# Weight tiles that alternate between 0 and 64 mod 128 bytes, and new start addresses for attention's and the ConvFFN's operands

## The chip, the cores and the metric

The kernel runs on one NeuronCore of a Trainium2 chip. The metric is device time in microseconds from the start of the program to its end; lower is better. Engines are named as in the profile: PE is TensorE (PEld its weight loads), DVE is VectorE, ACT is ScalarE, POOL is GpSimd, SP is SyncE.

## The reference

One block of a hybrid encoder, batch 1, 512 frames (T), width 1024 (D), float32:

```python
h = rms_norm(x, norm_mix_g)
proj = h @ w_in + b_in                                  # 1024 -> 4864 (38 blocks of 128)
y_a = rwkv7_branch(proj[..., :1792], ...) @ w_branch_a  # 8 heads of 64, delta-rule recurrence
y_b = rglru_branch(proj[..., 1792:2816], ...) @ w_branch_b  # conv4, gated linear recurrence
merged = sigmoid(g_a) * y_a + sigmoid(g_b) * y_b        # gates: the last 2048 columns of proj
x = x + merged @ w_mix_out
x = x + cross_attention(rms_norm(x, norm_x_g), rms_norm(mem, norm_mem_g), w_cq, w_ckv, w_co)  # 4 heads, 256 memory rows
u = rms_norm(x, norm_ffn_g) @ w_ffn_in                  # 1024 -> 2 x 2816
x = x + (gelu(causal_dwconv3(u[..., :2816])) * u[..., 2816:]) @ w_ffn_out
out = rms_norm(x, norm_final_g)
```

## The kernel before

Activations stand transposed: 128 channels on the partitions, 512 frames along them. Each matrix product is kept to near float32 accuracy with matmuls in the type fp32r: an operand is split into hi, its rounded value, and lo, what is left, and a product of one 128x128 weight block with one 128x512 (or 128x256) operand is three matmuls, hi by hi, hi by lo, lo by hi. The helper `mm3` (L165) issues them at L166, L167 and L168, so most matmuls of the profile carry those three lines and are told apart by the tile that they write. In each the weights (the first two arguments) are loaded into PE by a load of their own ahead of the matmul, and the second operand is moved through. The two loads for hi are both issued.

Weights come through one pool, `wp`. A group of eight 128x128 blocks (4 KB in each partition) is loaded from memory into a tile `wr` (four buffers) by SP, ACT copies it rounded into a tile `wh` and DVE writes the rest into a tile `wl`, three buffers of each. Three generators do this: `stream` (L100: w_in, w_ckv, the two branch products, mix, w_cq, w_co), `stream_quarters` (L124: w_ffn_in) and `out_weights` (L1315: w_ffn_out). A group's `wh` and `wl` always have the same buffer number, 0, 1 or 2.

The stages follow one another in this order, and the names are those of the tiles that PE writes: `k_ps` and `v_ps` (keys and values of the memory; in `v_ps` alone the weight tile is the moving operand and the activation m2 the stationary one), `in_ps` (the input projection, with the recurrences of both branches among it), `yb_ps` and `ya_ps` (branch products), `mix_ps`, then attention: `q_ps`, `sc_ps` (scores: q2 stationary, K2 moving, 256 columns), `prT_ps` (probabilities transposed), `o_ps` (V2 stationary, the probabilities prT moving), `co_ps` (the output product, o2 moving). In the ConvFFN both products are done with seven half-size products in place of eight: `fx_ps` and `fyz_ps` (first product), `ox_ps` and `oyz_ps` (second), all with 256 columns. Their moving operands are four tiles in the pool `big` (inside hq0 and hq1), and three, hr0 to hr2, in a pool `pr` that is placed from the far end of the memory ("right-hand"), behind a tile `pad` of 32 bytes. For the second product, go0 lies in the pool `pc`, go1 and go2 partly in the place of hq0 and hq1 and partly in that of hr0 and hr1.

Some sums of weight quarters that the seven-product scheme needs are made by accumulating DMAs on POOL's queue (`dS`, `dOs`), one behind chosen matmuls (`sum_behind`, L173).

A scheduler sets the order of instructions on each engine from the order of the program and priorities; tiles get addresses pool by pool, in the order in which they are made. Each tile starts at a multiple of 32 bytes. The start of a tile in bytes mod 128 is what the change moves. In the program before, with every matmul operand that matters here:

| operand | role | before | after |
|---|---|---|---|
| wh buffers 0, 1, 2 | weights | 0, 0, 0 | 0, 64, 0 |
| wl buffers 0, 1, 2 | weights | 0, 0, 0 | 64, 0, 64 |
| m2 | moving in k_ps, stationary in v_ps | 64 | 64 |
| hT2, yb2, ya2, mg2, hx | moving in in_ps, yb_ps, ya_ps, mix_ps, q_ps | 64 | 64 |
| q2, V2 | stationary in sc_ps, o_ps | 0 | 0 |
| K2, prT | moving in sc_ps, o_ps | 0 | 64 |
| o2 | moving in co_ps | 0 | 64 |
| hq0, hq1 | moving in fx_ps, fyz_ps | 64 | 64 |
| hr0, hr1, hr2 | moving in fx_ps, fyz_ps | 64 | 0 |
| go0, and the larger part of go1, go2 | moving in ox_ps, oyz_ps | 64 | 64 |
| the smaller part of go1, go2 (blocks 8 to 10) | moving in ox_ps, oyz_ps | 64 | 0 |

A block within a weight tile starts 512 bytes behind the one before, and a row of the other operands is a multiple of 128 bytes, so a tile's start sets the place mod 128 of every operand cut from it.

Of the kernel before, what the change touches and what calls it, by code (L numbers as in the profile page):

```python
# [17 lines left out]
P = 128  # L18
T = 512
# [39 lines left out]
def hybrid_block_kernel(ctx: ExitStack, tc: tile.TileContext, xT_d, mT_d, pv_d, cst_d, win_d, wk_d, wv_d,  # L59
# [37 lines left out]

    wdma, mdma, casts = [], [], []

    def stream(dram, name, between=None, order=None):  # L100

        for g in order or range(dram.shape[0]):
            with tc.high_priority():
                raw = wp.tile([P, 1024], F32, tag="wr", name=f"{name}_r{g}", bufs=4)
                n = 512 if len(wdma) < 2 else 1024
                ins = nc.sync.dma_start(raw, dram[g])
                if between is not None:
                    tc.keep_in_program_order(ins)
                    between(0)
                elif len(wdma) == 1:  # L110
                    tc.add_manual_dep(ins.ins, mdma[-1].ins.name, mybir.DependencyInfo(
                        mybir.DependencyClass.NoSync, mybir.DependencyReason.DATA), reason="order of the loads")
                wdma.append(ins)
                hi = wp.tile([P, 1024], F32R, tag="wh", name=f"{name}_h{g}")
                lo = wp.tile([P, 1024], F32R, tag="wl", name=f"{name}_l{g}")
                for o in range(0, 1024, n):
                    casts.append(S.copy(hi[:, o:o + n], raw[:, o:o + n]))  # L117
                    V.tensor_tensor(lo[:, o:o + n], raw[:, o:o + n], hi[:, o:o + n].bitcast(F32), ALU.subtract)  # L118
                    if between is not None and o == 0:
                        between(1)  # L120
                between = None
            yield hi, lo

    def stream_quarters(srcs, name):  # L124

        for g, src in enumerate(srcs):
            with tc.high_priority():
                raw = wp.tile([P, 2, T], F32, tag="wr", name=f"{name}_r{g}", bufs=4)
                wdma.append(nc.sync.dma_start(raw, src))
                hi = wp.tile([P, 2, T], F32R, tag="wh", name=f"{name}_h{g}")  # L130
                lo = wp.tile([P, 2, T], F32R, tag="wl", name=f"{name}_l{g}")
                S.copy(hi, raw)  # L132
                V.tensor_tensor(lo, raw, hi.bitcast(F32), ALU.subtract)  # L133
            for i in range(2):
                yield hi[:, i], lo[:, i]
# [917 lines left out]

    pb_ctx = ExitStack()
    pb = pb_ctx.enter_context(tc.tile_pool(name="pb", bufs=1, reuse_waits="tile"))
    rxc = pb.tile([P, 4], F32, name="rxc")
    nrx = pb.tile([P, 4], F32, name="nrx")
    pat_ctx = ExitStack()
    pat = pat_ctx.enter_context(tc.tile_pool(name="pat", bufs=1, space=PSUM, reuse_waits="tile"))
    psc = rw_ps("rxc_ps", pat, "sc", bufs=2)  # L1060
# [4 lines left out]
    V.tensor_scalar(rxc, rxc, 1.0 / 16, None, ALU.mult)  # L1065
    V.tensor_scalar(nrx, rxc, -1.0, None, ALU.mult)

    o2 = pb.tile([P, 2, KB, T], F32R, name="o2")
    pk_ctx = ExitStack()
    pk = pk_ctx.enter_context(tc.tile_pool(name="pk", bufs=1, reuse_waits="tile"))  # L1070
    K2 = pk.tile([P, 2, KB, NMEM], F32R, name="K2")
    V2 = pk.tile([P, 2, 2, D], F32R, name="V2")

    def load_kv(what, i):
# [24 lines left out]
        return q2  # L1099

    def attend(hd, q2):
        prT = pk.tile([P, 2, 2, T], F32R, tag="prT", name=f"prT{hd}", bufs=2)
        prps = [rw_ps(f"prT_ps{hd}_{i}", pat, "prT", bufs=2) for i in range(2)]
        for tt in range(4):
            sl = slice(tt * P, (tt + 1) * P)
            ps = rw_ps(f"sc_ps{hd}_{tt}", pat, "sc", bufs=2)
            for i in range(2):
                kb = 2 * hd + i
                PE.matmul(ps[:, :NMEM], q2[:, 0, i, sl], K2[:, 0, kb, :], start=(i == 0), stop=False)
                PE.matmul(ps[:, :NMEM], q2[:, 0, i, sl], K2[:, 1, kb, :], start=False, stop=False)  # L1110
                PE.matmul(ps[:, :NMEM], q2[:, 1, i, sl], K2[:, 0, kb, :], start=False, stop=(i == 1))
            st = pk.tile([P, 4], F32, tag="smst", name=f"smst{hd}_{tt}", bufs=4)
            V.tensor_reduce(st[:, 0:1], ps[:, :NMEM], AX.X, ALU.max)
            V.tensor_tensor(st[:, 1:2], st[:, 0:1], nrx[:, tt:tt + 1], ALU.mult)
            ex = pk.tile([P, NMEM], F32, tag="ex", name=f"ex{hd}_{tt}", bufs=3)
            S.activation(ex, ps[:, :NMEM], AF.Exp, scale=rxc[:, tt:tt + 1], bias=st[:, 1:2],
                         accum_out=st[:, 2:3])
            V.reciprocal(st[:, 3:4], st[:, 2:3])
            V.tensor_scalar(ex, ex, st[:, 3:4], None, ALU.mult)
            for i in range(2):  # L1120
                PE.transpose(prps[i][:, sl], ex[:, i * P:(i + 1) * P], ident)
        for i in range(2):
            S.copy(prT[:, 0, i, :], prps[i])
            V.tensor_tensor(prT[:, 1, i, :], prps[i], prT[:, 0, i, :].bitcast(F32), ALU.subtract)
        for i in range(2):
            kb = 2 * hd + i
            ps = rw_ps(f"o_ps{kb}", pat, "o")
            for n in range(2):
                cs = slice(kb * P, (kb + 1) * P)
                mm3(ps, V2[:, 0, n, cs], V2[:, 1, n, cs], prT[:, 0, n, :], prT[:, 1, n, :], n == 0, n == 1)  # L1130
            S.copy(o2[:, 0, kb, :], ps)
            V.tensor_tensor(o2[:, 1, kb, :], ps, o2[:, 0, kb, :].bitcast(F32), ALU.subtract)
# [18 lines left out]
    hq = [big.tile([P, 2, 2, 4, H], F32R, tag=f"act16_{i}", name=f"hq{i}") for i in range(2)]  # L1151
    hop = [hq[0][:, 0], hq[0][:, 1], hq[1][:, 0], hq[1][:, 1]]
    hop += [pr.tile([P, 2, 4, H], F32R, tag=f"hr{i}", name=f"hr{i}") for i in range(3)]
    pr.tile([P, 8], F32, name="pad")
    hop = dict(zip(("B11", "b1", "b2", "B22", "b3", "B21", "b4"), hop))
    ssf = cp.tile([P, T], F32, tag="ssq", name="ssf")

# [157 lines left out]
    def out_weights():  # L1315
# [9 lines left out]
        for g in range(0, len(flat), 8):  # L1325
            units = flat[g:g + 8]
            n = len(units) * P
            with tc.high_priority():
                raw = wp.tile([P, 1024], F32, tag="wr", name=f"wfo_r{g // 8}", bufs=4)
                k = 0  # L1330
                while k < len(units):
                    key, src, i = units[k]
                    e = k
                    while e < len(units) and units[e][0] == key and units[e][2] == i + e - k:
                        e += 1
                    nc.sync.dma_start(raw[:, k * P:e * P], src[:, i * P:(i + e - k) * P])
                    k = e
                hi = wp.tile([P, 1024], F32R, tag="wh", name=f"wfo_h{g // 8}")
                lo = wp.tile([P, 1024], F32R, tag="wl", name=f"wfo_l{g // 8}")
                S.copy(hi[:, :n], raw[:, :n])  # L1340
                V.tensor_tensor(lo[:, :n], raw[:, :n], hi[:, :n].bitcast(F32), ALU.subtract)  # L1341
            for k in range(len(units)):
                yield hi[:, k * P:(k + 1) * P], lo[:, k * P:(k + 1) * P]
# [186 lines left out]
```

## Time and profile before

| | |
|---|---|
| time, median of 3 runs | 892.87 us (892.58 to 893.33) |
| the profiled execution, from the first to the last instruction | 892.8 us |
| PE busy | 877.4 us (98%) |
| DVE busy | 685.2 us (77%) |
| ACT busy | 513.6 us (58%) |
| POOL busy | 132.5 us (15%) |
| granted TensorE clock, mean | 0.996 |

The profiled execution is one more run of the same program; no time of its own is listed beside its span of 892.8 us, which lies within 0.1 us of the median. Busy times of PE are those of a pipeline: a matmul's record is longer than the distance to the next one's start, so "busy 98%" says that PE had work, not how fast the work went. The distance from one matmul's start to the next (the spacing) says that, and the text reads it from timeline rows, which give start and length in microseconds, or from the count of matmuls in a window that PE fills.

### The profile page before, as it was taken

Reading aid. Unit: us, or ns where it says so; the run is one execution under the profiler, and the core shown is the slowest. Engines: PE = TensorE matmul, PEld = TensorE weight load, DVE = VectorE, ACT = ScalarE, POOL = GpSimd, SP = SyncE. Lnnn points to the kernel's source line nnn. Section 1 sums busy time; section 2 is a strip of 40 time slices with the busy share of each in tenths; the row PEclk is TensorE's granted clock in tenths of the full one; section 3 lists DMA queues with packets and bytes.
Section 4 is the critical chain, followed back from the end, with each engine's and each line's share of the span. In section 5 each row is a group of like instructions: output and inputs, shape, how many; then the busy total and the mean of one; then the engine's idle time right before and its main releaser. Section 6 shows DMA issues by size and latency. Waiting matters only on the chain.

```text
span 892.8 us, 15934 instructions
## 1 busy us (share of the span) xinstructions
PE 877.4 (98%) x6197; PEld 767.9 (86%) x6197; DVE 685.2 (77%) x1104; ACT 513.6 (58%) x783; POOL 132.5 (15%) x163
## 2 busy tenths in 40 slices
PE   8999999999999999999999999999999999999996
PEld 7878878888877677888888778999999999999996
DVE  6796598777967677675575578889888889999674
ACT  6575676634347676233554466766655656757563
POOL 0101222021102021001122111111111111211100
PEclk9999999999999999999999999999999999999999
DMA  7878899678997279758888958999999999998963
GB/s 268 307 253 215 206 228 233 187 203 233 262 227 156 72 203 249 220 166 229 218 234 183 197 137 185 260 275 271 265 255 294 263 297 275 244 276 220 261 202 94
DMA packets 97242, 201.37 MB, mean 226 GB/s; under 512 B 19536, under 2 KB 30928, under 8 KB 97104
## 3 DMA queue, kind: packets, MB, share of 16 engines
q1 hardware_dynamic: 62240, 118.57, 40.4%
q0 software_dynamic: 25504, 67.38, 36.9%
q10 hardware_dynamic: 9424, 14.42, 4.7%
q8 instruction: 48, 0.79, 0.4%
q14 instruction: 26, 0.21, 0.1%
HBM read 188.54 MB, written 78.12 MB: 299 GB/s over the span
## 4 chain that ended last, share of the span: by engine, by line
PE 91%; DVE 4%; DMA 2%; ACT 1%; issue 1%; DVEq 0%; ACTq 0%; SPq 0%
PE in_ps L167 7%; PE in_ps L166 7%; PE in_ps L168 7%; PE fx_ps L167 5%; PE fx_ps L166 5%; PE fx_ps L168 5%; PE fyz_ps L167 4%; PE fyz_ps L166 4%; PE fyz_ps L168 3%; PE ox_ps L166 2%; PE oyz_ps L166 2%; PE ox_ps L168 2%; PE oyz_ps L168 2%; PE oyz_ps L167 2%; PE ox_ps L167 2%; PE co_ps L167 2%
## 5 line engine op out<-in xcount | busy, mean ns | idle before, releaser
L132 ACT CAST wfi_h<-wfi_r 128x1024 fp32r<-128x1024 f32 x77 | 81.1, 1053 | 71.5 <-PE fx_ps L167 19.7
L168 PE MATMUL in_ps<-hT,win_l 128*128 128x512 f32 x304 | 121.3, 399 | 0.0
L167 PE MATMUL in_ps<-hT,win_h 128*128 128x512 f32 x304 | 121.0, 398 | 0.2 <-DVE hT L384 0.2
L166 PE MATMUL in_ps<-hT,win_h 128*128 128x512 f32 x304 | 120.6, 398 | 0.3 <-DVE pr L586 0.3
L133 DVE TENSOR_TENSOR wfi_l<-wfi_r,wfi_h 128x1024 fp32r<-128x1024 f32 x77 | 94.1, 1222 | 22.7 <-ACT wfi_h L132 22.4
L482 POOL DMA_DIRECT2D dS<-in_wfi x66 | 66.7, 1028 | 293.1 <-PE in_ps L166 102.3
L167 PEld LDWEIGHTS in_ps<-hT,win_h 128*128 128x128 f32 x304 | 57.1, 188 | 14.2 <-issue 0.7
L166 PEld LDWEIGHTS in_ps<-hT,win_h 128*128 128x128 f32 x304 | 57.1, 188 | 13.2 <-DVE pr L586 0.7
L168 PEld LDWEIGHTS in_ps<-hT,win_l 128*128 128x128 f32 x304 | 57.1, 188 | 13.1 <-issue 0.7
L518 POOL DMA_DIRECT2D dOs<-in_wfo x54 | 39.8, 784 | 181.5 <-PE fyz_ps L166 54.0
L118 DVE TENSOR_TENSOR win_l<-win_r,win_h 128x1024 fp32r<-128x1024 f32 x38 | 46.3, 1221 | 24.2 <-ACT win_h L117 20.7
L117 ACT CAST win_h<-win_r 128x1024 fp32r<-128x1024 f32 x38 | 39.9, 1050 | 41.1 <-PE in_ps L167 32.4
L1341 DVE TENSOR_TENSOR wfo_l<-wfo_r,wfo_h 128x1024 fp32r<-128x1024 f32 (+1 forms) x39 | 47.2, 1209 | 15.2 <-ACT wfo_h L1340 15.2
L1340 ACT CAST wfo_h<-wfo_r 128x1024 fp32r<-128x1024 f32 (+1 forms) x39 | 40.5, 1039 | 31.3 <-DMA wfo_r<-dOs 11.6
L168 PE MATMUL ox_ps<-go,wfo_l 128*128 128x256 f32 x176 | 49.1, 279 | 0.8 <-DVE wfo_l L1341 0.8
L166 PE MATMUL ox_ps<-go,wfo_h 128*128 128x256 f32 x176 | 49.2, 279 | 0.4 <-ACT wfo_h L1340 0.3
L166 PE MATMUL fx_ps<-hq,wfi_h 128*128 128x256 f32 x176 | 49.4, 280 | 0.0
L166 PE MATMUL fyz_ps<-hq,wfi_h 128*128 128x256 f32 x176 | 49.2, 280 | 0.0
L167 PE MATMUL fx_ps<-hq,wfi_h 128*128 128x256 f32 x176 | 49.2, 280 | 0.0
L167 PE MATMUL fyz_ps<-hq,wfi_h 128*128 128x256 f32 x176 | 49.2, 280 | 0.0
L167 PE MATMUL fx_ps<-hr,wfi_h 128*128 128x256 f32 x176 | 49.2, 280 | 0.0
L166 PE MATMUL fx_ps<-hr,wfi_h 128*128 128x256 f32 x176 | 49.2, 279 | 0.0
(432 smaller groups left out, 2704.9 us busy)
## 6 DMA issues: line engine op xcount, KB each, us to landing
dS<-in_wfi POOLq DMA_DIRECT2D x66, 512.0 KB, 7.8
wfi_r<-dS SPq DMA_DIRECT2D x44, 512.0 KB, 6.8
win_r<-in_win SPq DMA_DIRECT2D x38, 512.0 KB, 5.3
wfi_r<-in_wfi SPq DMA_DIRECT2D x33, 512.0 KB, 5.8
dS<-dS POOLq DMA_DIRECT2D x22, 512.0 KB, 5.7
dOs<-in_wfo POOLq DMA_DIRECT2D x12, 512.0 KB, 7.9
wk_r<-in_wk SPq DMA_DIRECT2D x8, 512.0 KB, 5.1
wv_r<-in_wv SPq DMA_DIRECT2D x8, 512.0 KB, 4.0
```

The source lines that it names most:

```text
L117: casts.append(S.copy(hi[:, o:o + n], raw[:, o:o + n]))
L118: V.tensor_tensor(lo[:, o:o + n], raw[:, o:o + n], hi[:, o:o + n].bitcast(F32), ALU.subtract)
L132: S.copy(hi, raw)
L133: V.tensor_tensor(lo, raw, hi.bitcast(F32), ALU.subtract)
L166: first = PE.matmul(ps, lh, rh, start=start, stop=False, **kw)
L167: PE.matmul(ps, lh, rl, start=False, stop=False, **kw)
L168: PE.matmul(ps, ll, rh, start=False, stop=stop, **kw)
L482: return lambda: nc.gpsimd.dma_start(s(out), src, **kw)
L518: yield lambda k=k, w=w, src=src: nc.gpsimd.dma_start(dO[n, m][:, k * P:(k + w) * P], src, **kw)
L1340: S.copy(hi[:, :n], raw[:, :n])
L1341: V.tensor_tensor(lo[:, :n], raw[:, :n], hi[:, :n].bitcast(F32), ALU.subtract)
```

## The change

It makes `wh` and `wl` tiles 64 bytes longer than what is used of them, so that the second of three buffers starts 64 bytes off the first and third, and the three `wl`, which follow the three `wh`, the other way round. The tiles of all pools that lie behind move up by 384 bytes, 0 mod 128. In attention, o2 moves by 320 bytes (two small tiles ahead of it, rxc and nrx, become one, rxn, behind prT), K2 and prT lie directly behind it, and rxn, 64 bytes, brings V2, the buffers for loading and q2 back to 0 mod 128; for room, the softmax's small tile of statistics `smst` has three buffers in place of four. V2 and what follows it come to lie 16 KB further up, on what the mix stage used. The right-hand pool's `pad` grows from 32 to 96 bytes, and hr0 to hr2 come to lie 64 bytes lower. PE's, POOL's and SP's instructions stay in the same order with the same waits; on DVE and ACT too the order stays, and a few waits of attention's first loads and casts name other tiles.

```diff
+    def weight_tile(tag, name):
+        return wp.tile([P, 1024 + 16], F32R, tag=tag, name=name)[:, 0:1024]
...
-                hi = wp.tile([P, 1024], F32R, tag="wh", name=f"{name}_h{g}")
-                lo = wp.tile([P, 1024], F32R, tag="wl", name=f"{name}_l{g}")
+                hi = weight_tile("wh", f"{name}_h{g}")
+                lo = weight_tile("wl", f"{name}_l{g}")
...
-                hi = wp.tile([P, 2, T], F32R, tag="wh", name=f"{name}_h{g}")
-                lo = wp.tile([P, 2, T], F32R, tag="wl", name=f"{name}_l{g}")
+                hi = weight_tile("wh", f"{name}_h{g}").rearrange("p (n f) -> p n f", n=2)
+                lo = weight_tile("wl", f"{name}_l{g}").rearrange("p (n f) -> p n f", n=2)
...
     pb = pb_ctx.enter_context(tc.tile_pool(name="pb", bufs=1, reuse_waits="tile"))
-    rxc = pb.tile([P, 4], F32, name="rxc")
-    nrx = pb.tile([P, 4], F32, name="nrx")
+    o2 = pb.tile([P, 2, KB, T], F32R, name="o2")
+    pk_ctx = ExitStack()
+    pk = pk_ctx.enter_context(tc.tile_pool(name="pk", bufs=1, reuse_waits="tile"))
+    K2 = pk.tile([P, 2, KB, NMEM], F32R, name="K2")
+
+    def probs(hd):
+        return pk.tile([P, 2, 2, T], F32R, tag="prT", name=f"prT{hd}", bufs=2)
+
+    prT0 = probs(0)
+    rxn = pk.tile([P, 16], F32, name="rxn")
+    rxc, nrx = rxn[:, 0:4], rxn[:, 4:8]
...
-    o2 = pb.tile([P, 2, KB, T], F32R, name="o2")
-    pk_ctx = ExitStack()
-    pk = pk_ctx.enter_context(tc.tile_pool(name="pk", bufs=1, reuse_waits="tile"))
-    K2 = pk.tile([P, 2, KB, NMEM], F32R, name="K2")
     V2 = pk.tile([P, 2, 2, D], F32R, name="V2")
...
-        prT = pk.tile([P, 2, 2, T], F32R, tag="prT", name=f"prT{hd}", bufs=2)
+        prT = probs(hd) if hd else prT0
...
-            st = pk.tile([P, 4], F32, tag="smst", name=f"smst{hd}_{tt}", bufs=4)
+            st = pk.tile([P, 4], F32, tag="smst", name=f"smst{hd}_{tt}", bufs=3)
...
-    pr.tile([P, 8], F32, name="pad")
+    pr.tile([P, 24], F32, name="pad")
...
-                hi = wp.tile([P, 1024], F32R, tag="wh", name=f"wfo_h{g // 8}")
-                lo = wp.tile([P, 1024], F32R, tag="wl", name=f"wfo_l{g // 8}")
+                hi = weight_tile("wh", f"wfo_h{g // 8}")
+                lo = weight_tile("wl", f"wfo_l{g // 8}")
```

## The prediction

> **What bounds the kernel now.** I read the page's shares first, then the chain that ended last, then the stages, then the distance from one matmul's start to the next.
>
> ```profile
> span 892.8 us, 15934 instructions
> PE 877.4 (98%) x6197; PEld 767.9 (86%) x6197; DVE 685.2 (77%) x1104; ACT 513.6 (58%) x783; POOL 132.5 (15%) x163
> PEclk9999999999999999999999999999999999999999
> PE 91%; DVE 4%; DMA 2%; ACT 1%; issue 1%; DVEq 0%; ACTq 0%; SPq 0%
> PE in_ps L167 7%; PE in_ps L166 7%; PE in_ps L168 7%; PE fx_ps L167 5%; PE fx_ps L166 5%; PE fx_ps L168 5%; PE fyz_ps L167 4%; PE fyz_ps L166 4%; PE fyz_ps L168 3%; PE ox_ps L166 2%; PE oyz_ps L166 2%; PE ox_ps L168 2%; PE oyz_ps L168 2%; PE oyz_ps L167 2%; PE ox_ps L167 2%; PE co_ps L167 2%
> ```
>
> The reader is to see that 91% of the path is matmuls at the full granted clock. So the time is a number of matmuls times their spacing, and whatever changes the spacing by 1% is worth some 8 us. The stages of the ConvFFN show what else would press if the matmuls ran closer:
>
> ```profile
> 564.00:783.00 219.00, 219.00 (x1859) 218.84 (x1858) 195.41 (x264) 137.59 (x198) 37.33 (x52) 1.00 0.94 271
> 783.00:852.00 69.00, 67.86 (x574) 67.21 (x573) 58.37 (x72) 43.32 (x57) 9.00 (x11) 1.00 0.90 251
> 852.00:877.00 25.00, 25.00 (x215) 24.73 (x214) 18.19 (x27) 14.06 (x22) 0.00 (x0) 1.00 0.60 184
> ```
>
> Columns: PE, PEld, DVE, ACT and POOL busy, clock, share of the DMA engines, GB/s. PE has no gap there, but the DMA engines are at 0.94 and DVE at 195 of 219 us: a stage 4% shorter would put the DMA at 0.98.
>
> The change adds no work. Order and kind of PE's, SP's and POOL's instructions stay; what differs is where operands lie. So the question is whether spacing depends on addresses. Timeline rows (start, length, engine, line, operation), first and last of undisturbed stretches with 512 columns:
>
> ```profile
> 399.64 0.39 PE L166 MATMUL mix_ps<-mg,wmix_h 128*128 128x512 f32 x1
> ...
> 401.47 0.39 PE L168 MATMUL mix_ps<-mg,wmix_l 128*128 128x512 f32 x1
> 520.00 0.39 PE L168 MATMUL co_ps<-o,wo_l 128*128 128x512 f32 x1
> ...
> 521.40 0.39 PE L168 MATMUL co_ps<-o,wo_l 128*128 128x512 f32 x1
> 56.02 0.39 PE L166 MATMUL v_ps<-wv_h,m 128*128 128x512 f32 x1
> ...
> 56.95 0.39 PE L167 MATMUL v_ps<-wv_l,m 128*128 128x512 f32 x1
> 57.41 0.40 PE L166 MATMUL in_ps<-hT,win_h 128*128 128x512 f32 x1
> ...
> 58.81 0.40 PE L166 MATMUL in_ps<-hT,win_h 128*128 128x512 f32 x1
> 68.41 0.39 PE L166 MATMUL in_ps<-hT,win_h 128*128 128x512 f32 x1
> ...
> 70.47 0.39 PE L166 MATMUL in_ps<-hT,win_h 128*128 128x512 f32 x1
> ```
>
> mix: 8 steps in 1.83 us, 229 ns; its moving operand starts at 64 mod 128 bytes, its weights at 0. co: 6 steps in 1.40 us, 233 ns; both at 0. v: 4 steps in 0.93 us, 233 ns; moving at 0, weights at 64. in_ps has the addresses of mix, yet its first tile steps at 233 ns (6 in 1.40 us), directly behind v, and after a short wait at 67 us at 229 ns (9 in 2.06 us). I read two things: there are two spacings, 4.4 ns apart, and which one holds depends on the addresses and also on how the stream got going. With 256 columns:
>
> ```profile
> 581.00:742.00 161.00, 161.00 (x1369) 1.00 0.94 274
> 843.20:865.20 22.00, 22.00 (x196) 1.00 0.71 218
> 870.00:882.00 12.00, 12.00 (x104) 1.00 0.26 87
> 842.66 0.38 PE L168 MATMUL ox_ps<-go,wfo_l 128*128 128x256 f32 x1 [0.75 <-DVE wfo_l L1341]
> ...
> 843.00 0.28 PE L167 MATMUL ox_ps<-go,wfo_h 128*128 128x256 f32 x1
> ...
> 844.13 0.28 PE L168 MATMUL ox_ps<-go,wfo_l 128*128 128x256 f32 x1
> 449.40 0.28 PE L1109 MATMUL sc_ps<-K,q 128*128 128x256 f32 x1
> ...
> 449.76 0.28 PE L1110 MATMUL sc_ps<-K,q 128*128 128x256 f32 x1
> ```
>
> The first three rows are windows with PE's busy time, count, clock and DMA share. A matmul that straddles an edge counts whole, so spacing is (window + 0.28) / count: 161.28 / 1369 = 117.8 ns for nearly all of the ConvFFN (moving 64, weights 0). From 843.00 to 844.13, behind a wait, 10 steps take 1.13 us: 113 ns, and that holds through 865 us (22.28 / 196 = 113.7, the count being whole). In the row for 870 to 882 it is 118 again, at a DMA share of only 0.26, so DMA load isn't what separates the two. Attention's scores, both operands at 0, step at 120 ns (3 in 0.36 us).
>
> **The parts and their cost.** Counts, one row per stage of 512 or 256 columns (three lines each, L166 to L168, of equal count):
>
> ```profile
> L168 PE MATMUL in_ps<-hT,win_l 128*128 128x512 f32 x304 | 121.3, 399 | 0.0
> L166 PE MATMUL q_ps<-hx,wq_h 128*128 128x512 f32 x64 | 25.3, 395 | 0.0
> L166 PE MATMUL mix_ps<-mg,wmix_h 128*128 128x512 f32 x64 | 25.1, 392 | 0.0
> L166 PE MATMUL co_ps<-o,wo_h 128*128 128x512 f32 x64 | 25.1, 395 | 0.0
> L166 PE MATMUL ya_ps<-ya,wba_h 128*128 128x512 f32 x32 | 12.5, 392 | 0.0
> L166 PE MATMUL o_ps<-prT,V 128*128 128x512 f32 x16 | 6.7, 420 | 0.0
> L166 PE MATMUL fx_ps<-hq,wfi_h 128*128 128x256 f32 x176 | 49.4, 280 | 0.0
> L166 PE MATMUL fx_ps<-hr,wfi_h 128*128 128x256 f32 x176 | 49.2, 279 | 0.0
> L166 PE MATMUL fyz_ps<-hq,wfi_h 128*128 128x256 f32 x176 | 49.2, 280 | 0.0
> L166 PE MATMUL fyz_ps<-hr,wfi_h 128*128 128x256 f32 x88 | 24.6, 279 | 0.0
> L166 PE MATMUL ox_ps<-go,wfo_h 128*128 128x256 f32 x176 | 49.2, 279 | 0.4 <-ACT wfo_h L1340 0.3
> L166 PE MATMUL oyz_ps<-go,wfo_h 128*128 128x256 f32 x132 | 37.1, 281 | 0.0
> ```
>
> A. Weights alternate, 512 columns, moving operand stays at 64: in 912, q and mix 192 each, ya and yb (as many) 96 each, 1488 in all. They have the shorter spacing now, so per matmul the bounds are 0 and +4.4 ns; a gain is left out because no row at 512 columns and full clock averages under 229. Now every weight load stands opposite to the moving operand; afterwards, with hi and lo of a group on different sides and the slots alternating, 4 of 9 loads share its side. I take the middle, +2.2 ns. in_ps holds 21% of the path, 187 us of its 912 x 0.229 = 209, so 90% of it counts: (576 + 0.9 x 912) x 2.2 ns = +3.1 us (0 to +6.1).
>
> B. Weights alternate, 256 columns: fx, fyz, ox, oyz, 2772 matmuls, about 200 of them at 113.3 already. Bounds per matmul: 113.3 (the stretch at 843 us) and 120 (the scores). The same addresses give both 117.8 and 113.3, and a run keeps what it fell into for 161 us while every matmul is like the last. Alternating sides end that sameness within each triple, so I expect time in both: 115.6, nearer to the ConvFFN's own rows than to the six-long runs of the scores. 2572 x -2.2 = -5.7 us, the 200 lose 0.4, the 168 of the K projection (same shape, moving 64) gain 0.4: -5.7 us (-12.0 to +7.4). The right-hand pool's move to 0 changes which half of those products' loads share a side, not how many to within a few per cent; I give it nothing (within the same bounds).
>
> C. Attention: the scores' K2 and the probabilities go to 64 against weights (q2, V2) that stay at 0, and o2 to 64 against alternating wo. o and co, 240 matmuls, from 233.3 to the middle: -0.5 us; 96 scores from 120 to 117.8: -0.2 us. Together -0.7 (-1.3 to 0). v, 96 matmuls, has its moving operand alternate instead and is at the longer spacing: 0 (-0.4 to 0).
>
> D. The rest: one buffer fewer of the softmax's statistics frees in VectorE's own order and costs nothing, since `ex` beside it already has three; rxc and nrx in one tile issue the same operations. V2 moves 16 KB up, onto buffers of the mix stage, so its first cast also waits for those. It runs behind a load that is waited for anyway and ahead of o_ps by many us; without that cover it would cost PE a wait of the cast's length, 1 us:
>
> ```profile
> 444.56 1.05 ACT L1084 CAST V<-kvV 128x1024 fp32r<-128x1024 f32 x1 [0.65 <-DMA kvV<-dV]
> ```
>
> Sum: +3.1 - 5.7 - 0.7 = -3.3 us. The profiled span, 892.8, plus under 0.1 around it, stands at the median of the runs, 892.87; so **889.5 us**.
>
> **A rule against it.** The Trainium skill, "TensorE: Matmul & The Clock Gate", Part 2 (step by step), says that PE reads stationary and moving operands through two independent ports, so that loading the next weights takes nothing from the running matmul. By that, addresses change nothing and the sum is 0, 892.9 us. The trace speaks against it: co and mix, same shape and clock, differ by 4.4 ns. It stands as the second rival.
>
> **Rivals.**
> 1. Each pairing keeps its own price, in the stages ahead of the ConvFFN: 4 of 9 loads cost 4.4 ns in A, 1397 x 0.44 x 4.4 = +2.7; the 200 short ones go to 117.8, +0.9; C gives -0.6; B nothing. 895.9 us, slower. For it: co and v are longer wherever the pairing isn't "moving 64, weights 0", and the scores at 0 and 0 are no faster than 117.8. Against: in_ps at 57 us is long with the good pairing. It decides when the ConvFFN's mean spacing, 117.4 now, stays above 116.6.
> 2. Spacing follows the start of a run and not the addresses, and A, B and C cancel or stay: 892.9, no change. For it: in_ps and ox have two spacings with one set of addresses. Against: co keeps 233 for 33 us.
> 3. The ConvFFN falls into 113.3 for good and A stays at 229: -12.0 - 1.3, or 879.5, of which the DMA at 0.98 and DVE at 0.93 give some back: 882. For it: 22 us of exactly that. Against: of all the ConvFFN's restarts behind waits one led there.
>
> **How the numbers follow.** Forecast (886 to 891) 0.38; rival 3 (880 to 886) 0.14; rival 2 0.18; rival 1 (895 to 900) 0.30. Under 0.2%, 1.8 us, a measurement of this kernel tells nothing from no change. Faster is the forecast and rival 3, 0.52; same 0.18; slower 0.30. With signs on both sides, the forecast's own range is 886 to 891; the range for 8 in 10, 882.5 to 897, leaves out the far half of rival 3 and the top of rival 1, where A goes to 233 throughout with B at rest.
>
> **What would show it.** A: steps of mix, ya, yb and in_ps between 229 and 233 ns. B: the count in a 161 us window of fx and fyz near 1395 (115.6) instead of 1369; 1423 is rival 3, 1369 or fewer rival 1. C: co below 233 ns. A wait of PE on wfi_l or wfi_h in the ConvFFN, absent now, would show that supply has become the bound. The forecast is wrong if spacing isn't moved by halves but every matmul steps at one of the two values, or at a third one that no row here shows.

## The result, and the profile after

The changed kernel takes 897.32 us (median of 4 runs, 896.46 to 898.55) where the kernel before takes 892.84 (4 runs, 892.58 to 893.33): a ratio of 1.0044, interval 1.0029 to 1.0059 (the quotient of the two medians is 1.0050; the ratios given here with intervals are estimates of their own and need not be that quotient). It is slower by 0.44%, near the time of the prediction's rival 1, and not the forecast.

The page of the changed kernel, its lines on the span, PE's busy time, the granted clock and the chain by engine:

```profile
span 895.9 us, 15937 instructions
PE 881.5 (98%) x6197; PEld 769.1 (86%) x6197; DVE 685.5 (77%) x1104; ACT 513.5 (57%) x783; POOL 132.5 (15%) x163
PEclk9999999999999999999999999999999999999998
PE 90%; DVE 4%; DMA 3%; ACT 1%; issue 1%; DVEq 0%; ACTq 0%
```

The same work at the same clock in a span 3.1 us longer. This execution took 897.68 us, 1.8 more than its span. So the profiled execution before, with a span of 892.8, stood some 1.7 us over its median, and the two traces account for 3.1 of the 4.5 us between the medians; the other 1.4 lie in how executions differ.

The ConvFFN's three windows, in the same columns as before, then one of 161 us (PE alone):

```profile
564.00:783.00 219.00, 219.00 (x1857) 218.62 (x1857) 194.47 (x262) 138.08 (x200) 36.55 (x51) 1.00 0.94 270
783.00:852.00 69.00, 68.85 (x585) 68.65 (x584) 60.16 (x73) 44.78 (x59) 10.50 (x14) 1.00 0.91 256
852.00:877.00 25.00, 25.00 (x210) 24.73 (x209) 18.20 (x28) 13.91 (x23) 0.00 (x0) 1.00 0.64 196
590.00:751.00 161.00, 161.00 (x1371) 1.00 0.94 275
```

In 161 us 1371 matmuls: 161.28 / 1371 = 117.6 ns, where 117.8 stood before and 115.6 was forecast. The last of the windows by stage has lost five matmuls (210 against 215): the stretch at 113 ns is gone.

Timeline rows of the changed kernel (start, length): the first and the last of mix_ps, which is 192 matmuls in a row, and between them each 24th, with which a new buffer of weights begins; two rows of co_ps with 76 between them; two of in_ps with 20 between them:

```profile
393.55 0.40 PE L169 MATMUL mix_ps<-mg,wmix_h 128*128 128x512 f32 x1
...
399.14 0.39 PE L169 MATMUL mix_ps<-mg,wmix_h 128*128 128x512 f32 x1
...
404.67 0.40 PE L169 MATMUL mix_ps<-mg,wmix_h 128*128 128x512 f32 x1
...
410.31 0.40 PE L169 MATMUL mix_ps<-mg,wmix_h 128*128 128x512 f32 x1
...
437.96 0.40 PE L171 MATMUL mix_ps<-mg,wmix_l 128*128 128x512 f32 x1
523.63 0.39 PE L171 MATMUL co_ps<-o,wo_l 128*128 128x512 f32 x1
...
541.53 0.39 PE L170 MATMUL co_ps<-o,wo_h 128*128 128x512 f32 x1
68.10 0.39 PE L170 MATMUL in_ps<-hT,win_h 128*128 128x512 f32 x1
...
72.94 0.39 PE L170 MATMUL in_ps<-hT,win_h 128*128 128x512 f32 x1
```

mix: 44.41 us / 191 = 232.5 ns, from 229. co: 17.90 / 77 = 232.5, from 233. in_ps: 4.84 / 21 = 230.5 here, 232.0 over the whole stage. None is one of two values any more: in mix_ps steps from 225 to 240 ns, and two of 260, stand in one stream. By buffer, 24 steps each, mix takes 5.59, 5.53 and 5.64 us, 233, 230 and 235 ns, and so round again.

Adding up the distances between starts stage by stage in both traces gives, after less before: in_ps +2.0, q +1.6 (of it 1.3 in one wait among its matmuls), mix +0.7, ya +0.4, yb +0.3; k_ps +0.2; v, scores, o and co -0.6; fx, fyz, ox, oyz -1.1. That is +3.5, against a span 3.1 us longer.

The wait in q is one of PE for the softmax (`prT_ps` for DVE's `ex`). ACT had come late to the softmax's exponentials, because its cast of K, ahead of them, waited for K's load. The rows of that cast, before and after, then the first cast of V after (the prediction shows it before) and the wait:

```profile
455.97 1.05 ACT L1084 CAST K<-kvK 128x1024 fp32r<-128x1024 f32 x1 [0.65 <-DMA kvK<-dK]
460.28 1.05 ACT L1092 CAST K<-kvK 128x1024 fp32r<-128x1024 f32 x1 [2.01 <-DMA kvK<-dK]
447.76 1.05 ACT L1092 CAST V<-kvV 128x1024 fp32r<-128x1024 f32 x1 [1.00 <-DMA kvV<-dV]
PE prT_ps L1129 <- DVE ex L1127: 1.3, 1, 1.3
```

In the trace of the kernel before, V's cast starts 0.02 us after the landing of its load; in this one it starts 0.43 us after it, with two instructions that only wait ahead of it on ACT. The next load of V is issued with that cast, and the load of K when that load has landed. K's load itself took 7.8 us here and 6.8 before.

### The profile page after: what moved, and what is told of

Its sections match the earlier page's. It is cut to its first block, busy times and chain, and to the rows that moved or that the text cites. A ratio compares the mean times of both kernels' runs of the same rounds, so it can differ in the third digit from the quotient of the medians.

```text
span 895.9 us, 15937 instructions
## 1 busy us (share of the span) xinstructions
PE 881.5 (98%) x6197; PEld 769.1 (86%) x6197; DVE 685.5 (77%) x1104; ACT 513.5 (57%) x783; POOL 132.5 (15%) x163
## 4 chain that ended last, share of the span: by engine, by line
PE 90%; DVE 4%; DMA 3%; ACT 1%; issue 1%; DVEq 0%; ACTq 0%
PE in_ps L170 7%; PE in_ps L169 7%; PE in_ps L171 7%; PE fx_ps L170 5%; PE fx_ps L169 5%; PE fx_ps L171 5%; PE fyz_ps L170 3%; PE fyz_ps L171 3%; PE fyz_ps L169 3%; PE ox_ps L169 2%; PE ox_ps L171 2%; PE ox_ps L170 2%; PE oyz_ps L171 2%; PE oyz_ps L170 2%; PE oyz_ps L169 2%; PE co_ps L169 2%
## 5 line engine op out<-in xcount | busy, mean ns | idle before, releaser
L169 PE MATMUL fx_ps<-hq,wfi_h 128*128 128x256 f32 x176 | 49.6, 282 | 0.0
L171 PE MATMUL fx_ps<-hq,wfi_l 128*128 128x256 f32 x176 | 49.4, 280 | 0.0
L171 PE MATMUL fyz_ps<-hq,wfi_l 128*128 128x256 f32 x176 | 49.4, 280 | 0.0
L171 PE MATMUL fx_ps<-hr,wfi_l 128*128 128x256 f32 x176 | 49.3, 280 | 0.0
```

What stands on the lines that cost most here:

```text
L169: first = PE.matmul(ps, lh, rh, start=start, stop=False, **kw)
L171: PE.matmul(ps, ll, rh, start=False, stop=stop, **kw)
```

## The experiments

Places are given mod 512 bytes from here on, as the compiled programs have them. In the kernel before all weight blocks start at 128 and the moving operands of k, in, yb, ya, mix, q and the ConvFFN at 448. Times and ratios are against runs of the kernel before on the same chip (its medians there were 893.65 to 894.24). The first five take the change apart. The four after them were made to tell two theories apart: S, that weights which switch sides cost; P, that a pairing on the same side mod 128 costs. What was expected of each run stands ahead of its result.

**The parts alone.** The changed kernel with weight tiles of the old length (attention at 64, hr at 0):

```diff
-        return wp.tile([P, 1024 + 16], F32R, tag=tag, name=name)[:, 0:1024]
+        return wp.tile([P, 1024], F32R, tag=tag, name=name)[:, 0:1024]
```

> The change with the weight tiles back at 4096 bytes, so all weights at 0 mod 128; attention's operands at 64 and hr0 to hr2 at 0 stay as the change has them. Theory 1 (each weight load that starts on the moving operand's side costs the 512-column matmuls ahead of the ConvFFN, and the ConvFFN gains nothing): mix, ya and in_ps back at 229 ns, co from 233 to 229, so about 1 us under before, 891.5 to 892. Theory 2 (the loss comes from attention's moved tiles and their waits, or from the right-hand pool): still near 897. Theory 3 (the spacing follows how a run of matmuls got started, not the addresses): 892.8 with mix at 229 and co at 233.

895.13 us, ratio 1.0015 (1.0005 to 1.0026). Mix is back at 228.9, co at 229.5; yet there is no gain, since the products from hr step at 120.0 ns.

The weights alone (the kernel before with `weight_tile`, and `smst` with three buffers for room):

> The program before with the longer, alternating weight tiles alone (and three buffers of the softmax statistics, for room); attention's operands and hr at their old places mod 128. Theory 1: +4.5 to +6 us, 897.5 to 899, because attention's part is not there to win its 1 us; mix near 232 ns. Theory 2: 892.8. Theory 3: within 1 us of before.

896.84 us, ratio 1.0033 (1.0021 to 1.0045); mix 232.3, in 232.0, the ConvFFN 117.4 to 117.6. Most of the loss is here.

Attention alone (the changed kernel with weight tiles of the old length and `pad` of 8):

> The program before with attention's new layout alone (o2, K2, prT at 64, V2 and q2 at 0), weights all at 0, hr at 64. Theory 1: co and o from 233 to 229 ns, 240 x 4.4 ns = 1.1 us, and some 0.2 us in the scores: 891.5. Theory 2: slower than before by 1 to 4 us, with a new wait near 440 to 450 us. Theory 3: 892.8.

893.35 us, ratio 0.9997 (0.9988 to 1.0006). The rows of its co_ps, with 146 between them:

```profile
520.71 0.39 PE L171 MATMUL co_ps<-o,wo_l 128*128 128x512 f32 x1
...
554.35 0.39 PE L171 MATMUL co_ps<-o,wo_l 128*128 128x512 f32 x1
```

33.64 / 147 = 228.8 ns: the part does what it says, 192 x 4.5 = 0.9 us. In this trace PE waits 1.7 us for the softmax among the matmuls of q, as in the changed kernel, and in time no gain shows.

The right-hand pool alone:

```diff
-    pr.tile([P, 8], F32, name="pad")
+    pr.tile([P, 24], F32, name="pad")
```

> The program before with the right-hand pool's pad at 96 bytes alone, so that hr0 to hr2 (3 of 7 products of the ConvFFN's first half) are at 0 with weights at 0. Theory 1: 256-column spacing does not depend on the side, 117.8 ns in all products, 892.8. If 256 columns behave like 512 (a load on the moving side is longer by 4.4 ns), 792 matmuls cost 3.5 us: 896.3. If they behave the other way, 889.3.

895.72 us, ratio 1.0027 (1.0012 to 1.0041). Two rows of hr products with 68 between them:

```profile
586.05 0.28 PE L168 MATMUL fx_ps<-hr,wfi_l 128*128 128x256 f32 x1
...
594.33 0.28 PE L168 MATMUL fx_ps<-hr,wfi_l 128*128 128x256 f32 x1
```

8.28 / 69 = 120.0 ns, while hq's stay at 117.8. 792 products of hr and 144 of the second product's smaller parts by 2.2 ns would be 2.1 of the 2.4 us.

Then the whole change without that part (`pad` back to 8):

> The changed kernel with hr0 to hr2 back at 64. Theory 1 (where the weights alternate, the right-hand pool's side decides nothing, as the prediction put it): 897.3 us +- 0.4, a ratio of 1.005 to the kernel before, products from hr at 117.5 to 118. Rival (its +2.4 us alone is carried into the change): 894.9, a ratio of 1.002, and fx, fyz from hr shorter by 1 to 2 ns than in the changed kernel.

897.94 us, ratio 1.0042 (1.0027 to 1.0057), as the change itself. What costs 2.4 us where the weights stand still costs nothing where they move: in the first product hr at 448 steps at 117.2 to 117.7 there, and hr at 384 at 117.7 to 117.8 in the changed kernel.

**Sides without alternation.** Tiles of 64 bytes ahead of `wh`, between `wh` and `wl`, or behind `wl`, in the kernel before; for all weights at 64 the first and the last:

```diff
+                if len(wdma) == 1:
+                    wp.tile([P, 16], F32, tag="pad0", name="pad0", bufs=1)
                 hi = wp.tile([P, 1024], F32R, tag="wh", name=f"{name}_h{g}")
                 lo = wp.tile([P, 1024], F32R, tag="wl", name=f"{name}_l{g}")
+                if len(wdma) == 1:
+                    wp.tile([P, 16], F32, tag="pad2", name="pad2", bufs=1)
```

> The program before with all weight tiles, hi and lo, at 64 mod 128, so that weights and moving operands lie on the same side in every stage of the dense products; nothing alternates (co: moving 0, weights 64; scores and o as before). Theory P (a pairing on the same side has a price of its own: +4.4 ns at 512 columns, as in co, +2.2 at 256, as hr at 0 showed): steady 233 and 120 ns, 1397 x 4.4 + 2940 x 2.2 ns = +12.6 us, some 905 us. Theory S (what costs is that the side switches between hi and lo or between groups, not the pairing): steady 229 and 118, within 1 us of before.

900.37 us, ratio 1.0068 (1.0051 to 1.0085): 232.4 at 512 columns, 118.7 from hq, 120.0 from hr. Nothing switches, and it is the slowest so far: S is out as the whole cause. P has the sign and half of the size.

hi at 0, lo at 64 (tiles between and behind):

> The program before with every wh at 0 and every wl at 64, so that hi and lo switch sides within each triple and all groups are alike; moving operands at 64. Theory P, price by price: 1 load in 3 on the moving side, 512 columns 230.4 ns, 256 columns 118.5, +2.0 + 2.1 = 897. Theory S: as the groups of this kind in the changed kernel, 233.3 ns at 512 and 117.3 at 256: 1397 x 4.4 - 2772 x 0.4 = +5 us, 898.5; and if the steady form of 256 columns is the 115.7 that a quarter of those triples had, near 893.

896.41 us, ratio 1.0028 (1.0019 to 1.0038): mix 231.1, fx and fyz near 118 from hq, close to P.

The last tile alone, so that the moving operands stand at 0:

> The program before with everything behind the weight tiles moved up by 64 bytes: moving operands at 0 with weights at 0 in the dense products (K, V, input projection, branches, mix, q) and in the ConvFFN but for hr (64); co gets moving 64 against weights 0, scores and o 64 against 64. Theory P: 512 columns at 233.3 ns but co at 229, +6.1 - 0.8; 256 columns at 120 but for hr's products, 1980 x 2.2 = +4.4: 903. Theory S: within 1 us of before.

899.78 us, ratio 1.0064 (1.0043 to 1.0084): mix 233.3. This fits P too, 3 us short of its time, but for one stage. o2 stands at 64 here, on the other side of its weights at 128, and its 19 steps between these rows take 4.44 us, 233.7 ns:

```profile
529.71 0.40 PE L168 MATMUL co_ps<-o,wo_h 128*128 128x512 f32 x1
...
534.15 0.39 PE L169 MATMUL co_ps<-o,wo_h 128*128 128x512 f32 x1
```

hi at 64, lo at 0 (tiles ahead and between):

> The program before with every wh at 64 and every wl at 0; moving operands at 64. Theory P: 2 loads in 3 on the moving side, 512 columns 231.9 ns, 256 columns 119.3: +4.1 + 4.2, 902. Theory S: as the groups of this kind in the changed kernel, 230.4 and 118.1 ns: +2 + 1 us, 897.

897.14 us, ratio 1.0048 (1.003 to 1.0067): 233.1 at 512 columns, and 117.2 on average at 256, a little under the 117.8 of before. The time is S's, but the spacings are neither theory's.

I took that last figure for a gain to be had and combined it with the attention part: weight tiles `wh` 128 bytes longer, from which the ConvFFN takes its hi weights 64 bytes in.

```diff
+    def weight_tile(tag, name, off=0):
+        return wp.tile([P, 1024 + (32 if tag == "wh" else 0)], F32R, tag=tag, name=name)[:, off:off + 1024]
```

> The changed kernel's attention part alone (weights at 0 there, o2, K2 and prT at 64), with one thing more: in the ConvFFN alone the hi weights start at 64 and the lo weights at 0; hr0 to hr2 stay at 64. The candidate for a version that beats both. Theory P (a pairing has its price, and with 256 columns hi at 64 and lo at 0 steps at 117.2 on average, as with constant sides in an earlier run): 2772 x -0.6 = -1.7 us in the ConvFFN, -0.9 in o and co, -0.2 in the scores: 890.0 us, or a ratio of 0.997 to the kernel before, with fx and fyz at 117.2 and in_ps, mix at 229. Rival (the 117.2 of that run was the chance of its restarts): 117.8 in the ConvFFN, and as the attention part alone gave no gain in time, 0.999 to 1.000.

895.88 us, ratio 1.0025 (1.0012 to 1.0037): wrong by both theories. The first and the last row of its mix_ps:

```profile
391.58 0.39 PE L169 MATMUL mix_ps<-mg,wmix_h 128*128 128x512 f32 x1
...
435.76 0.40 PE L171 MATMUL mix_ps<-mg,wmix_l 128*128 128x512 f32 x1
```

44.18 / 191 = 231.3 ns. Every weight of this stage is at 0 mod 128 and its moving operand at 64, as before; only the buffers of `wh` are 128 bytes further apart. With co of the run that moves the moving operands to 0, P falls as well: the side mod 128 isn't what is priced.

**Does a break in the rhythm draw a new spacing?** The attention part alone, with 22 short matmuls whose columns the next matmul starts afresh:

```diff
+        if nudge:
+            PE.matmul(out[:, 0:nudge], wh[:, 0:P], b[:, 0, 0, 0:nudge], start=True, stop=True)
```

> The attention part alone, with 22 short matmuls put in between products of the ConvFFN, 40 to 166 columns wide in steps of 6 (each writes columns that the next matmul starts afresh). Asks what sets 113.3 or 117.8 ns with one and the same addresses. Theory R (a stretch keeps the spacing with which it got going; anything that breaks its rhythm draws anew): of the 22 stretches of some 84 matmuls several, by the restarts behind waits so far about 1 in 5, step at 113.3, and the others at 117.8; 4 x 84 x 4.4 = 1.5 us gained, 22 x some 0.07 = 1.5 us lost: 1.000 of the kernel before. Theory W (only an idle gap draws anew, since then the next weights are loaded ahead of time): all stretches at 117.8, and the time is the kernel before's plus 1.5 us, 1.0015.

896.7 us, ratio 1.0033 (1.0019 to 1.0047). All 22 stretches step at 117.8. Theory R is out. Of theory W the spacings came, but not that only an idle gap draws anew: at other distances, below, 113 ns also came with a change of operand. The short ones cost more than I thought, some 112 ns each by the starts around them, 2.5 us in all.

**The distance.** The weights left where they are, and everything behind them moved up by a tile of 128 to 384 bytes, in one run of 32 (here 256), so that the distance from weights to moving operands takes each value in turn while nothing alternates. Theory M prices the side mod 128, theory D the distance mod 512. hr, at 320, is the control, and its products step at 117.8 in all six:

```diff
                 lo = wp.tile([P, 1024], F32R, tag="wl", name=f"{name}_l{g}")
+                if len(wdma) == 1:
+                    wp.tile([P, 64], F32, tag="shift", name="shift", bufs=1)
```

> The kernel before with a tile of 128 bytes behind the weights: the moving operands start 448 bytes (mod 512) behind the weights instead of 320; hr stays at 320; smst has three buffers. Sides mod 128 as before (weights 0, moving 64). Theory M (side mod 128): 228.9 at 512 columns, 117.8 at 256, 892.9 us, ratio 1.000. Theory D (distance mod 512): 233.7 at 512, as co_ps had at this distance: 1397 x 4.6 = +6.4 us, 899.3, ratio 1.007; co at distance 0 at some 230.

> The same with 192 bytes: distance 0, both operands on one side mod 128; hr stays at 320. Theory M: 233.3 at 512 columns, 118.7 in the products from hq and go, as with moving operands at 0: 899.8 us, ratio 1.007. Theory D: 230 to 231 and 118.3, as o_ps and the scores had at distance 0: 1397 x 1.6 + 1840 x 0.5 = +3.2, 896.1, ratio 1.0035.

> The same with 256 bytes: distance 64, opposite sides mod 128; hr stays at 320. Theory M: as the kernel before, 228.9 and 117.8, 892.9 us, ratio 1.000. Theory D: no constant case at this distance but v_ps at 231.9: +3 ns x 1397 = +4.2, 897.1, ratio 1.005.

> The same with 320 bytes: distance 128, one side mod 128; hr stays at 320. Theory M: 233.3 and 118.7, 899.8 us, ratio 1.007. Theory D: v_ps had 232.3 at this distance, and in mixed runs 256 columns stepped at 117.3: 1397 x 3.4 - 1840 x 0.5 = +3.8, 896.7, ratio 1.004.

> The kernel before with a tile of 384 bytes behind the weights: distance 192 from weights to moving operands (mod 512), opposite sides mod 128; hr stays at 320; smst has three buffers; co at distance 256. Theory M (side mod 128): 228.9 and 117.8, 892.9 us, ratio 1.000; co at 233.3 as it is on one side. Theory D (distance): v_ps had 233.3 at this distance: 1397 x 4.4 = +6.1, 899.0, ratio 1.007.

> The same with 32 bytes: distance 352, between the kernel before's 320 (228.9 ns) and 384 (233.3 ns); hr stays at 320. If only whole 64-byte places count, one of those two values throughout: 892.9 or 899.0 us. If the distance counts by the byte, a value between: near 231, 896.

First and last rows of mix_ps at distance 448, 0 and 64, one fence each:

```profile
395.11 0.39 PE L168 MATMUL mix_ps<-mg,wmix_h 128*128 128x512 f32 x1
...
439.67 0.39 PE L170 MATMUL mix_ps<-mg,wmix_l 128*128 128x512 f32 x1
```

```profile
389.14 0.39 PE L168 MATMUL mix_ps<-mg,wmix_h 128*128 128x512 f32 x1
...
432.44 0.39 PE L170 MATMUL mix_ps<-mg,wmix_l 128*128 128x512 f32 x1
```

```profile
391.27 0.39 PE L168 MATMUL mix_ps<-mg,wmix_h 128*128 128x512 f32 x1
...
434.99 0.39 PE L170 MATMUL mix_ps<-mg,wmix_l 128*128 128x512 f32 x1
```

44.56, 43.30 and 43.72 us by 191 steps: 233.3, 226.7 and 228.9 ns. At 448 the sides are those of the kernel before and the price is the long one (against M); at 0 both are on one side and the spacing is the shortest of all. Products from hq at distance 0, 94 rows between these two:

```profile
611.86 0.29 PE L168 MATMUL fx_ps<-hq,wfi_h 128*128 128x256 f32 x1
...
623.26 0.28 PE L170 MATMUL fyz_ps<-hq,wfi_l 128*128 128x256 f32 x1
```

11.40 / 95 = 120.0 ns: what is best for 512 columns is worst for 256. The 161 us window at distance 448, and then at 192:

```profile
590.00:751.00 161.00, 161.00 (x1369) 1.00 0.95 276
```

```profile
590.00:751.00 161.00, 161.00 (x1395) 1.00 0.95 279
```

117.8 and 115.6 ns. At 192 the products from hq step at 113.3 to 114.4 from 584 us on, after a wait, and those from hr at 117.8 between them; behind each product from hr those from hq come back to 113.

Theory D fails in its prices too: at 64 it expected 231.9 and not 228.9, at 0 from 230 and not 226.7. Its unit, the distance, is what was kept. Put together after the fact, for every kernel whose weights stand still, distances that differ by 256 give nearly the same spacing (within 1 ns in the row of 128):

| distance mod 256 | 512 columns, ns | 256 columns, ns | seen in (distance mod 512) |
|---|---|---|---|
| 0 | 226.7 | 120.0 | 0 moved; co at 256 where the shift was 384 (227 to 228); hr at 256 |
| 64 | 228.9 | 117.8, stretches at 113.3 | the kernel before at 320; 64 moved; attention alone, co at 320; v at 64 where the shift was 128 or 384 |
| 128 | 232.4 or 233.3 | 118.6 | 128 moved; all weights at 64, moving at 0 and co of before, all at 384 |
| 192 | 233.3 | 117.8 or 113.3 | 448 and 192 moved; v of before at 192 |
| 96 | 233.3 | 120.0 | 352 moved |

The table is one of long streams. o_ps, at distance 0 in the kernel before, comes in runs of 12 matmuls, and its steps are 231 ns on average and not 226.7.

Times, by distance: at 64 it is 893.24 us, 0.9986 (0.9968 to 1.0004), no change, as the row of the table says. At 448 it is 894.11, 1.0008 (0.9989 to 1.0027), and at 192 895.22, 1.0015 (0.9999 to 1.0032), where theory D expected some +6 us. The dearer stages came (in, yb, ya, mix and q +4.6 us together at 448), but co, at distance 0 and 256 in these two, steps at 227 to 228, v at 229, and the ConvFFN took 6.4 us less in the trace at 192. That trace is of the shortest of ten executions (891.99 us, to 899.53), so it may be that 113 ns isn't had in each; the others have no trace. At 0 it is 894.72, 1.0000 (0.9986 to 1.0014): 512 columns gain what 256 lose. At 128 it is 899.30, 1.0052 (1.0037 to 1.0067), and at 352 903.26, 1.0109 (1.0081 to 1.0136), the dearest.

**The table put to use.** Each product at the distance that the table prices lowest: in, yb, ya, mix, q, v, o and co at 0, the whole ConvFFN at 192. The two large tiles are cut in two ways, and the other operands get room ahead of them:

```diff
+    def act16(i, name, dt=F32R, ffn=False):
+        n, dense_at, ffn_at = ((48, 0, 48), (16, 16, 0))[i]
+        o = ffn_at if ffn else dense_at
+        return big.tile([P, KB * T + n], dt, tag=f"act16_{i}", name=name)[:, o:o + KB * T]
...
+                    shift.append(wp.tile([P, 48], F32, tag="shift", name="shift", bufs=1))
...
+    rxc, nrx = shift[0][:, 0:4], shift[0][:, 8:12]
...
-    pr.tile([P, 8], F32, name="pad")
+    pr.tile([P, 40], F32, name="pad")
...
+    pc.tile([P, 112], F32, name="gpad", bufs=1)
```

> The kernel before with each moving operand set at the distance from its weights that the shifted kernels priced lowest, mod 256 bytes: 0 for the products with 512 columns (226.7 ns in place of 228.9, v and co 227.5 in place of 233.3), 192 for all of the ConvFFN (113.3 to 114.4 ns in place of 117.8), weights unchanged. The two large tiles get 192 and 64 bytes more, from which the stages with 512 columns take one part and the ConvFFN another; 192 bytes lie behind the weights (rxc and nrx are put there), 448 ahead of go0, 128 more in the right-hand pool's pad; smst has three buffers. Theory T (a table by distance mod 256): (576 + 0.9 x 912) x -2.2 = -3.1 us, v 96 x -6 = -0.6, co 192 x -5.8 = -1.1, ConvFFN 2572 x -3.9 = -10.0, the K projection at distance 0 goes to 120: +0.4. Sum -14.4: 878.5 us, ratio 0.984; up to 3 us less if the DMA engines, at 0.94 in the ConvFFN, make PE wait there. Rival 1 (113 depends on how a stretch starts and not on the distance): the ConvFFN stays at 117.8, -4.4: 888.5, ratio 0.995. Rival 2 (the stages with 512 columns do not hold 226.7 where hi and lo lie at 0 and at 256 bytes): -10.5, ratio 0.988.

888.48 us (886.08 to 891.31, 6 runs) against 893.72, ratio 0.9945 (0.9927 to 0.9963): faster than both kernels, near rival 1. Its page, mix_ps, and two windows of the ConvFFN:

```profile
span 886.5 us, 15935 instructions
389.55 0.39 PE L168 MATMUL mix_ps<-mg,wmix_h 128*128 128x512 f32 x1
...
432.84 0.39 PE L170 MATMUL mix_ps<-mg,wmix_l 128*128 128x512 f32 x1
590.00:751.00 161.00, 161.00 (x1369) 1.00 0.95 274
785.00:821.00 36.00, 36.00 (x320) 1.00 0.89 233
```

mix steps at 43.29 / 191 = 226.7, and co at 227.5: the part of the table for 512 columns is confirmed by use, but for o_ps, at 230 on average. The ConvFFN runs at 117.8 from 551 to 782 us, but for a few matmuls, then, behind a wait in ox_ps, at 36.28 / 320 = 113.4 until near 862 us. With the same distance as in the run at 192, then, the products drew the other of the two spacings for their first 230 us. At 113.3 there too it would save some 1850 x 4.4 = 8 us more. What draws it wasn't found.

## Why the prediction was wrong

**Where it failed: step B's reasoning on sameness.** It took 117.8 for a rhythm into which like matmuls fall and which alternating sides would break, 115.6 ns, -5.7 us. The window of 161 us holds 1371 matmuls and not 1395. B as a whole gave -0.9 with k_ps, and owes even that to 1.6 us less of waiting in ox_ps, whose spacing rose from 116.0 to 117.6. Of the 6.8 us between the forecast -3.3 and the +3.5 of the traces, 4.8 are B's, 1.9 lie in the stages of A. Breaking the rhythm doesn't bring 113 (22 short matmuls, none did); what brought it in these traces followed a wait, or a change of operand at distance 192 or 448. And alternating weights don't mix two prices in B; they go round four rows of the table, and with the weights alone moved the ConvFFN stays at 117.4 to 117.6.

**Behind it: the unit was wrong from the start.** The change's own words and my reading spoke of places mod 128. At 4160 bytes a tile, `wh` starts at 128, 192, 256 and `wl` at 320, 384, 448; against moving operands at 320 the distances mod 256 are 192, 128, 64 and 0, 192, 128. By the table that is, with two loads in three for hi, (2 x 231.5 + 230.8) / 3 = 231.3 ns at 512 columns; measured 232.0 in in_ps and 232.5 in mix. The kernel before stood at distance 64 in all those stages, the second best row, and the mean of the rows visited lies above it. But the sum is right only as an average. By buffer the table gives 231.1, 232.7 and 230.1 ns, and mix has 233, 230 and 235, the other way round; hi 0, lo 64 has 231.1 where it gives 233, and hi 64, lo 0 has 233.1 where it gives some 231.5. So that the averages agree to 1 ns is in part luck. The table holds for operands at rest; what a load costs among others at other distances is left open. That alternating weights lift these stages to 232 ns is shown by the run with the weights alone, and by the one without them.

**A: sign right, size a little short, mechanism wrong.** +2.2 ns and +3.1 us were forecast; yb, mix and ya rose by 2.8 to 4.4, in_ps by 2.6 between its waits, and the stages together by 5.0 us, 1.3 of them the wait in q. The middle was taken between two prices of which 4 loads in 9, those on the moving operand's side, would pay the longer. But all loads on the other side step at 233.3 at distance 448, and all on the same side at 226.7 at distance 0; and a gain, left out because no row stood under 229, was there to be had. Of the table's rows two stand 3.5 to 4.4 ns above the one of the kernel before and one 2.2 below, and all are visited.

**B's sentence on the right-hand pool** ("I give it nothing") holds inside the change, by the run without it. As a statement on the part it was wrong: alone it costs 0.27%, since distance 256 is the row at 120.0. The reason given, that the halves only swap, held because the weights pass through all rows wherever hr stands.

**C: right in sign.** -0.7 forecast, -0.2 measured in co, o and the scores, and -0.5 in v, to which it gave nothing; 0.4 of that is less waiting. With weights that stand still co gains 4.5 ns (attention alone), since 448 - 128 is distance 64; inside the change its weights go round as well, and 232.5 is left. **D was put at nothing, and isn't quite.** V's first cast starts 0.43 us behind the landing of its load in each of the six traces with the attention part, and 0.02 to 0.03 behind it in the other 14. PE doesn't wait for V2 itself. But the loads behind that cast are held back with it, and in three of the six PE waits 1.3 to 2.5 us for the softmax; in the 14 it does so once, 0.7 us. How much of that is D's and how much the slower load of K isn't shown. The prediction also says of the ConvFFN's rows that PE has no gap there. The second has 67.86 us of 69.00; the rest are waits in ox_ps, of which the changed kernel's execution has fewer.

**The sum's anchor.** The profiled execution was not "under 0.1" from the median. By the later runs, where time and span stand side by side, 1.8 us lie around the span, so it was a long one. The -3.3 us were set against the median all the same, so this moved the forecast by nothing, but it hid how much executions of one program differ: those of the kernel before, over all chips, by more than the whole effect (889.3 to 897.1 us).

**The rivals.** Rival 1, 895.9, came nearest, and its time is in part luck: it gave A 2.7 us for loads on the same side, which is not what is priced, and nothing to waits. It was right that B gains nothing; "decides when the ConvFFN's mean spacing stays above 116.6" was the right test. Rival 2 is contradicted at 512 columns: the same program moved by 64 bytes steps at 233.3 or at 226.7. At 256 columns it had a point, two spacings with one set of addresses. The Trainium skill, "TensorE: Matmul & The Clock Gate", Part 2 (step by step), has weights and moving operand come through two independent ports. What the prediction drew from it, that addresses change nothing, is contradicted by the same 6.6 ns. Rival 3's 113 ns exists, but isn't had by this change.

## What to carry to other kernels

In a kernel like this one, where fp32r matmuls with a weight load each fill PE, look at the distance from the weights' start to the moving operand's start mod 256 bytes, and sweep it with one pad tile while nothing alternates: 3% of a stage's time lay in it here, for the price of a few hundred bytes. Which distance is best differs between 512 and 256 columns, so a shift of everything at once hides the gain (distance 0: ratio 1.0000), and the part must be set stage by stage. Read the effect from starts of long runs without waits, since times of this kernel differ by 0.3% and more from execution to execution.

## What was not expected of the hardware

- Spacing with a weight load ahead of each matmul came in a few values, again and again: 226.7, 228.9, 232.4 and 233.3 ns at 512 columns, 113.3, 117.8, 118.6 and 120.0 at 256, at full granted clock, for operands at rest. In long streams they go with the distance mod 256 bytes between the two operands, at the five distances tried. Why, no trace here shows.
- At distances 64 and 192 the 256-column matmuls have two spacings, 117.8 and 113.3, with the same addresses. In the last kernel each held, for 230 us and for 80 us, and the 113 ns outlasted two short waits; in the kernel moved to 448 the products from hq held 113 for two products, until a wait, and 117.8 in the later rounds of fx and fyz. It may be what makes executions of one program differ: those of the kernel before ranged from 889.3 to 897.1 us. That wasn't shown.
- A short matmul of 40 to 166 columns between long ones cost some 112 ns (108 to 116) whatever its width: at 40 columns it started 27 ns ahead of the next matmul, which then stepped at 204.
